# The first feed-forward layer's modulation made in four quarters of the features, and the tokens loaded ahead of the weights on one queue

## The chip, the cores and the metric

One core of one Trainium2 chip. The metric is the device time of one execution in microseconds (us), the median of a few runs; the profile shows one further execution of the same program, with its own time. Engines as the profile names them: PE multiplies matrices (PEld is its weight load, which overlaps), DVE and ACT work on vectors, POOL is the general-purpose engine, SP only issues transfers (DMAs). Each engine takes its instructions strictly in program order, and they meet through semaphores.

## The reference, cut to what matters

Two layers, three sublayers each, on 384 tokens (two tiles of 128 latent tokens, one tile of 128 context tokens) of 1024 features. Only the very first sublayer's start is touched:

```python
mod = silu(cond) @ w_ada[i] + b_ada[i]            # cond = c (latent) or c_ctx (context)
h = rmsnorm(x, norm_pre) * (1 + scale) + shift     # scale, shift: 1024 columns each of mod
a, b = split(h @ w_in)                             # w_in: 1024 x 5632
out = (silu(a) * b) @ w_out                        # w_out: 2816 x 1024
```

So before the first product of the kernel can run, the modulation needs 2048 columns of `w_ada` (8 MB), the tokens (1.5 MB), their norms, and their transposes.

## The kernel before, in words

**Weights.** All weights stream through one ordered list `chunks` of 512 KB pieces, issued by SP (`w_dma`, L172) into a rotating set of raw buffers (`raw_of`; the first `NE` chunks rotate over ten buffers, the later ones over the three `raws`). Chunks in the set `plain` (the `w_ada` ones) are used as they are. Every other chunk is split by `w_split`: ACT makes a rounded high part `wh` (L198), DVE (or POOL, where `ws["eng"]` is `G`) makes the low part `wl` (L199). There are five `wh`/`wl` pairs (`NW`). `take` hands out the next chunk and splits it if that has not been done; `prefetch(n)` splits up to n chunks ahead. A raw buffer's next transfer is issued once its last reader is done; SP's queue is in order, so it waits there.

**Products.** A product is made of three matmuls of 384 columns (high x high, high x low, low x high: L451 to L453, or L461 to L466). A chunk of the first feed-forward layer holds 4 blocks of 128 features and 256 output columns, that is 8 products or 24 matmuls. Chunk (g, kp) is output group g, features 0 to 511 for kp 0 and 1, features 512 to 1023 for kp 2 and 3; kp 0 and 2 carry `a`, kp 1 and 3 carry `b`. The text also names the first eight by the names in the changed code: f00, f01, f02, f03 are group 0 with kp 0 to 3, and f10 to f13 group 1.

**The start (`start`).** Tokens come by POOL's queue (L1407). Each tile is squared (ACT L365), gets its factor from POOL (L358, L359), is scaled by DVE (L1471) and transposed on PE (`lay`, L434). `gather` (L1428) multiplies a `w_ada` chunk with the two condition vectors; the sums lie in four strips of a PSUM bank, which ACT copies (L1430); `spread` (L1437) adds the strips and turns them into columns, and DVE finishes scale and shift (L1443, L1447). `modulate_first` applies them: DVE scales (L1458), ACT makes the high part of `hT` (L1463), DVE the low part (L1467). This is done in two halves of the features: 8 `w_ada` chunks, features 0 to 511, three feed-forward chunks' products, with the other 8 `w_ada` chunks in between (`between`), then features 512 to 1023 and the other products of the first two groups. From the ninth chunk on the layer runs chunk after chunk.

**Background work.** The modulations of the later sublayers are made by DVE on the side: `pace` is called 50 times in the first layer, and in all 80 units (`ada_unit`, DVE L245 and L247, fed by POOL's transfers) are spread evenly over the calls. A "kind" is 16 units; two calls after its last unit PE sums it with four matmuls against ones (`ada_step`, L272). Five kinds belong to the first layer. `pace` is called once per chunk in the first matrix product from where the loop goes on after `between`, and once per 128 rows (k) of the second one (`project_out`). In there, k = 0 to 13 run for all tokens, the last eight chunks are kept and used tile by tile (`block`), and five splits of weights more than usual are done from k = 9 on.

## Time and profile before

| | |
|---|---|
| time, median of 3 runs | 1585.67 us (1583.9 to 1587.08) |
| the profiled execution: time, span | 1587.23 us, 1585.5 us |
| PE busy | 1549.3 us, 98% of the span |
| DVE, ACT, POOL busy | 66%, 41%, 10% |
| end of the first eight feed-forward chunks | 71.98 us from the span's start |

Time from the span's start is used throughout. A row of the timeline gives start, length, engine, line, operation, output <- inputs, shape and count; what stands in brackets is the idle time before it and what ended it. Matmuls overlap, so the pace of a series is read from the starts, not from the lengths.

### The profile page before, as it was taken

How to read it: one execution, taken by the hardware profiler on the slowest of the kernel's cores; microseconds unless marked ns; L12 is line 12 of the kernel's file. 1: busy time of each engine (PE TensorE's matmuls, PEld its weight loads, DVE VectorE, ACT ScalarE, POOL GpSimd, SP SyncE). 2: the span in 40 equal slices, each digit the busy share in tenths (PEclk: the TensorE clock that was granted, in tenths of full speed). 3: DMA queues.
4: the chain of work that ended last, by engine and by line, in shares of the span. 5: the costliest groups of instructions: out<-in, count | busy, mean ns of one | idle time of the engine just before them, and what ended most of it. 6: DMA issues, size and time to landing. Idle time of an engine off the chain costs nothing.

```text
span 1585.5 us, 22547 instructions
## 1 busy us (share of the span) xinstructions
PE 1549.3 (98%) x8798; PEld 1414.8 (89%) x8798; DVE 1046.4 (66%) x1388; ACT 651.6 (41%) x1118; POOL 161.7 (10%) x308
## 2 busy tenths in 40 slices
PE   6999999998999999999999999999999999999997
PEld 4899998887879999988999998899999889999985
DVE  3787788577756777785688889666666764333452
ACT  3423233365745322334523233356655443323441
POOL 1111111000011111120111111110000110000000
PEclk9999999999999999999999999999999999999999
DMA  8777667342224766665377776634333335433321
GB/s 307 245 242 219 221 214 239 120 146 81 67 94 138 218 216 206 207 215 180 114 235 228 227 236 229 227 106 134 101 113 100 121 113 163 130 126 127 131 96 40
DMA packets 164091, 264.50 MB, mean 167 GB/s; under 512 B 10432, under 2 KB 122144, under 8 KB 163984
## 3 DMA queue, kind: packets, MB, share of 16 engines
q1 hardware_dynamic: 140592, 187.27, 36.4%
q0 software_dynamic: 22864, 75.36, 14.8%
q8 instruction: 69, 1.13, 0.3%
q10 hardware_dynamic: 528, 0.43, 0.1%
q14 instruction: 38, 0.31, 0.1%
HBM read 260.01 MB, written 3.01 MB: 166 GB/s over the span
## 4 chain that ended last, share of the span: by engine, by line
PE 92%; DVE 4%; ACT 2%; issue 1%; DMA 0%; POOL 0%; DVEq 0%; POOLq 0%; ACTq 0%
PE pb L451 14%; PE pb L452 14%; PE pb L453 14%; PE pb L461 14%; PE pb L463 13%; PE pb L466 13%; PE pb L963 1%; PE pb L272 1%; PE pb L953 1%; PE pb L923 1%; PE pb L1132 1%; DVE slot L247 1%; PE pb L434 1%; DVE wl L199 1%; PE pb L1428 1%
## 5 line engine op out<-in xcount | busy, mean ns | idle before, releaser
L198 ACT ACTIVATE wh<-raw 128x1024 fp32r<-128x1024 f32 x247 | 259.8, 1058 | 413.2 <-PE pb L466 254.8
L461 PE MATMUL pb<-hT,wh 128*128 128x384 f32 (+1 forms) x1248 | 410.2, 332 | 0.0
L199 DVE TENSOR_TENSOR wl<-raw,wh 128x1024 fp32r<-128x1024 f32 x245 | 298.5, 1223 | 167.7 <-ACT wh L198 167.2
L463 PE MATMUL pb<-hT,wl 128*128 128x384 f32 (+1 forms) x1248 | 406.5, 329 | 0.0
L247 DVE SCALAR_TENSOR_TENSOR slot<-araw,sc,slot 128x1024 f32<-128x1024 f32 x224 | 281.5, 1279 | 0.0
L466 PE MATMUL pb<-hT,wh 128*128 128x384 f32 (+1 forms) x1248 | 259.8, 329 | 0.0
L461 PEld LDWEIGHTS pb<-hT,wh 128*128 128x128 f32 x1248 | 234.8, 188 | 6.2 <-issue 5.9
L463 PEld LDWEIGHTS pb<-hT,wl 128*128 128x128 f32 x1248 | 234.9, 188 | 0.2
L466 PEld LDWEIGHTS pb<-hT,wh 128*128 128x128 f32 x1248 | 215.8, 188 | 0.0
L451 PE MATMUL pb<-wh,gh 128*128 128x512 f32 x384 | 150.6, 392 | 0.2 <-DVE dump L282 0.2
L452 PE MATMUL pb<-wl,gh 128*128 128x512 f32 x384 | 149.6, 389 | 0.0
L453 PE MATMUL pb<-wh,gl 128*128 128x512 f32 x384 | 149.5, 389 | 0.0
L233 POOL DMA_DIRECT2D araw<-in_w_ada_dram x128 | 68.7, 537 | 578.0 <-DVE slot L247 480.6
L451 PE MATMUL pb<-hT,wh 128*128 128x384 f32 x352 | 119.7, 340 | 4.9 <-ACT hT L1463 4.9
L452 PE MATMUL pb<-hT,wh 128*128 128x384 f32 x352 | 119.0, 338 | 0.2 <-DVE hT L1467 0.2
L453 PE MATMUL pb<-hT,wl 128*128 128x384 f32 x352 | 118.6, 337 | 0.0
L199 DVE TENSOR_TENSOR wl<-araw,wh 128x1024 fp32r<-128x1024 f32 x52 | 63.6, 1224 | 68.3 <-ACT wh L198 68.3
L451 PE MATMUL pb<-wh,hT 128*128 128x512 f32 (+1 forms) x258 | 94.3, 365 | 1.1 <-ACT sgn L1242 0.9
L453 PE MATMUL pb<-wh,hT 128*128 128x512 f32 (+1 forms) x258 | 90.7, 352 | 0.0
L452 PE MATMUL pb<-wl,hT 128*128 128x512 f32 (+1 forms) x258 | 90.6, 351 | 0.0
L451 PEld LDWEIGHTS pb<-wh,gh 128*128 128x128 f32 x384 | 72.1, 188 | 19.4 <-issue 3.4
L453 PEld LDWEIGHTS pb<-wh,gl 128*128 128x128 f32 x384 | 72.1, 188 | 15.2
(242 smaller groups left out, 2177.8 us busy)
## 6 DMA issues: line engine op xcount, KB each, us to landing
raw<-in_w_ffn_in_dram SPq DMA_DIRECT2D x155, 512.0 KB, 4.4
araw<-in_w_ada_dram POOLq DMA_DIRECT2D x128, 512.0 KB, 4.4
raw<-in_w_ffn_out_dram SPq DMA_DIRECT2D x76, 512.0 KB, 4.2
raw<-in_w_rec_in_dram SPq DMA_DIRECT2D x21, 512.0 KB, 3.6
araw<-in_w_ffn_in_dram SPq DMA_DIRECT2D x21, 512.0 KB, 3.5
araw<-in_w_rec_in_dram SPq DMA_DIRECT2D x19, 512.0 KB, 3.7
slot<-dsc POOLq DMA_DIRECT2D x24, 256.0 KB, 5.2
raw<-in_w_qkv_dram SPq DMA_DIRECT2D x12, 512.0 KB, 4.1
```

What stands on the lines that cost most here:

```text
L198: S.activation(out=h, in_=r, func=AF.Copy)
L199: ws["eng"].tensor_tensor(out=lo, in0=r, in1=h.bitcast(F32), op=ALU.subtract)
L233: G.dma_start(out=araw[j % NA], in_=w_ada[kd[0], (j % 8) * P:(j % 8 + 1) * P, acol(kd):acol(kd) + 1024])
L247: V.scalar_tensor_tensor(out=acc[v], in0=src, scalar=s_, in1=acc[v], op0=ALU.mult, op1=ALU.add)
L272: T.matmul(out=bank[32 * r:32 * r + 32, :], lhsT=ones, rhs=acc[v][:, 512 * h:512 * h + 512], start=True, stop=True, skip_group_check=True,)
L434: T.transpose(bks[half][:, k * P:(k + 1) * P], src[:, kk * P:(kk + 1) * P], ident)
L451: T.matmul(out=out, lhsT=a[0], rhs=b[0], start=start, stop=False, skip_group_check=True)
L452: T.matmul(out=out, lhsT=a[0], rhs=b[1], start=False, stop=False, skip_group_check=True)
L453: T.matmul(out=out, lhsT=a[1], rhs=b[0], start=False, stop=stop, skip_group_check=True)
L461: T.matmul(out=out, lhsT=a[0], rhs=b[0], start=start, stop=False, skip_group_check=True)
L463: T.matmul(out=out, lhsT=x, rhs=y, start=False, stop=False, skip_group_check=True)
L466: T.matmul(out=out, lhsT=x, rhs=y, start=False, stop=stop, skip_group_check=True)
```

## The change

The modulation is made in four quarters of 256 features. A quarter needs four `w_ada` chunks of 256 columns (two for scale, two for shift; a chunk is now four blocks of 128 rows by 256 columns), which come as one `gather` each of four matmuls of 256 columns. The order of the chunks is: four `w_ada` chunks, f00, f01; four, f10, f11; four, f02, f03; four, f12, f13. `unit` runs two feature blocks of one output tile (6 matmuls); every quarter of the features has 8 units. `NE` goes from 18 to 22. The tokens are loaded by SP's queue ahead of all weights. `between` holds the written order, the gates of both groups included, and the loop goes on with n = 8 where it went on with n = 3.

```diff
-NE = 18
-PLAIN = tuple(range(8)) + tuple(range(10, 18))
+NE = 22
+PLAIN = tuple(6 * q + i for q in range(4) for i in range(4))
...
+    order = add_ffn(0, 0)
+    early_chunks = []
+    for q in range(4):
         for kind in (1, 0):
-            for q in range(4):
-                col = kind * 1024 + half * 512
-                chunks.append(av[0][:, 2 * q:2 * q + 2, col:col + 512])
...
+            col = kind * 1024 + 256 * q
+            early_chunks += [av[0][:, 4 * h:4 * h + 4, col:col + 256] for h in range(2)]
+        early_chunks += chunks[4 * (q % 2) + 2 * (q // 2):][:2]
+    chunks[0:8] = early_chunks
...
+            def unit(gi, s, m, w, kq):
+                wv = [a.rearrange("p (k n) -> p k n", k=4) for a in w]
+                ms = slice(m * P, m * P + P)
+                group = []
+                for k in (2 * kq, 2 * kq + 1):
+                    group.append((bank(gi, m, s)[:, 0:TOK], (wv[0][:, k % 4, ms], wv[1][:, k % 4, ms]), (hT[:, :, 0, k, :], hT[:, :, 1, k, :]),
+                                  k == 0, k == KD - 1))
+                mm3s(group, "a")
...
-                    between(fill)
+                    between(unit, gate)
                     prefetch()
-                    n = 3
+                    n = 8
...
-        w_dma()
         SP.dma_start(out=cf[:, 0:P + 2], in_=cst_f[:, 0:P + 2])
         for t in range(2):
-            G.dma_start(out=x[t], in_=x_sample[0, t * P:(t + 1) * P, :])
-        G.dma_start(out=x[2], in_=x_prompt[0])
+            SP.dma_start(out=x[t], in_=x_sample[0, t * P:(t + 1) * P, :])
+        SP.dma_start(out=x[2], in_=x_prompt[0])
         w_ahead()
...
+        def gather(q, i, ahead=3):
+            kind, h = 1 - i // 2, i % 2
             (w,) = take()
+            for k4 in range(4):
+                r = slice(32 * k4, 32 * k4 + 2)
+                T.matmul(
+                    out=PB[7][r, 256 * kind:256 * kind + 256], lhsT=sc[:, :, 4 * h + k4], rhs=w[0][:, 256 * k4:256 * k4 + 256],
+                    start=h == 0, stop=h == 1, skip_group_check=True,
+                )
+            if i == 3:
+                S.activation(out=mrw[q % 2], in_=PB[7], func=AF.Copy)
...
+        def between(unit, gate):
+            ws["eng"] = G
+            (f00,) = take()
+            ws["eng"] = V
+            modulate_first(0)
+            (f01,) = take()
+            laid(1)
+            for s, w in ((0, f00), (1, f01)):
+                for m in range(2):
+                    unit(0, s, m, w, 0)
+            for i in range(4):
+                gather(1, i, 0)
+            (f10,) = take()
+            unit(1, 0, 0, f10, 0)
+            spread(1)
+            unit(1, 0, 1, f10, 0)
             modulate_first(1)
+            (f11,) = take()
+            unit(1, 1, 0, f11, 0)
+            for m in range(2):
+                unit(0, 0, m, f00, 1)
+            for i in range(4):
+                gather(2, i, 0)
+            for m in range(2):
+                unit(0, 1, m, f01, 1)
+            spread(2)
+            for s, m, w in ((0, 0, f10), (0, 1, f10), (1, 0, f11)):
+                unit(1, s, m, w, 1)
+            (f02,) = take()
+            modulate_first(2)
+            (f03,) = take()
+            for s, w in ((0, f02), (1, f03)):
+                for m in range(2):
+                    unit(0, s, m, w, 2)
+            for i in range(4):
+                gather(3, i, 0)
+            (f12,) = take()
+            for m in range(2):
+                unit(1, 0, m, f12, 2)
+            spread(3)
+            modulate_first(3)
+            for kq in range(2):
+                unit(1, 1, 1, f11, kq)
+            (f13,) = take()
+            w_split(24, 12)
+            for s, w in ((0, f02), (1, f03)):
+                for m in range(2):
+                    unit(0, s, m, w, 3)
+            gate(0, TOK)
+            w_split(26, 18)
+            for m in range(2):
+                unit(1, 1, m, f13, 2)
+            for s, w in ((0, f12), (1, f13)):
+                for m in range(2):
+                    unit(1, s, m, w, 3)
+            gate(1, TOK)
```

Three places of the changed order are shown. Lines of the changed program lie three below (helpers) or up to 17 below (`start`) those of before: L195 and L196 are the old L198 and L199, L1411 the old L1428, L1416 the old L1430, L1425 the old L1437, L1454 the old L1463, L244 the old L247, L269 the old L272.

**First place: ACT after the second set of gathers.** Before, where PE has begun the second half's gathers (L1430 is the copy of the gathered sums, L198 a high part of weights):

```order
L198 ACTIVATE wh_98<-raw_95 128x1024 [waits DMAHW7_49]
L1481 ACTIVATE slot_113<-pb_67 128x4x128
L1430 ACTIVATE slot_111<-pb_71 128x512 [waits PE_49]
L198 ACTIVATE wh_99<-raw_94 128x1024 [waits DMAHW0_49]
L1430 ACTIVATE slot_111<-pb_70 128x512 [waits PE_49,Activation_49]
L198 ACTIVATE wh_100<-raw_95 128x1024 [waits DMAHW1_49]
L198 ACTIVATE wh_101<-raw_96 128x1024 [waits DMAHW2_49]
```

And with the change, after the first quarter's `hT` (wh_99 is f10, wh_100 is f11):

```order
L195 ACTIVATE wh_98<-araw_108 128x1024 [waits DMAHW6_49]
L1472 ACTIVATE slot_113<-pb_67 128x4x128
L1416 ACTIVATE slot_111<-pb_71 128x512 [waits PE_49]
L195 ACTIVATE wh_99<-raw_96 128x1024 [waits DMAHW3_49]
L1454 ACTIVATE hT<-slot_112 128x2x128 [waits DVE_49]
L1454 ACTIVATE hT<-slot_114 128x128 [waits DVE_49]
L1454 ACTIVATE hT<-slot_112 128x2x128 [waits DVE_49]
L1454 ACTIVATE hT<-slot_114 128x128 [waits DVE_49]
L195 ACTIVATE wh_100<-slot_115 128x1024 [waits DMAHW4_49]
```

The high part of f10 stands right behind the copy that waits for PE's gathers, and that of f11 behind the second quarter's `hT`; before, two more copies of sums and three high parts stood together ahead of the second half's `hT`.

**Second place: PE at the last gathers, and SP's transfers for them.** Before, PE between two halves (wh_99 is the third chunk, raw_94 holds it):

```order
L1428 MATMUL pb_70<-araw_108,sc 2x512 x2
L1437 MATMUL pb_71<-cf,slot_111 128x2 x4
L1428 MATMUL pb_70<-araw_109,sc 2x512 x2
L1428 MATMUL pb_70<-gbr,sc 2x512 x2
L451 MATMUL pb_68<-hT,wh_99 128x384
L452 MATMUL pb_68<-hT,wh_99 128x384
L453 MATMUL pb_68<-hT,wl_104 128x384
```

With the change, PE at the fourth quarter (wh_98 is f12, which is loaded into raw_95):

```order
L1411 MATMUL pb_71<-raw_94,sc 2x256 x4
L1411 MATMUL pb_71<-raw_95,sc 2x256 x4
L1411 MATMUL pb_71<-raw_96,sc 2x256 x4
L1411 MATMUL pb_71<-slot_115,sc 2x256 x4
L458 MATMUL pb_68<-hT,wh_98 128x384
L460 MATMUL pb_68<-hT,wh_98 128x384
```

And SP's queue there (the first four are the fourth quarter's `w_ada` chunks, then f12, f13 and the ninth chunk):

```order
L169 DMA raw_94<-in_w_ada_dram 128x4x256 [waits DMAHW3_49,PE_49]
L169 DMA raw_95<-in_w_ada_dram 128x4x256 [waits DMAHW4_49,PE_49]
L169 DMA raw_96<-in_w_ada_dram 128x4x256 [waits DMAHW5_49,DVE_49]
L169 DMA slot_115<-in_w_ada_dram 128x4x256 [waits DMAHW6_49,DVE_49]
L169 DMA raw_95<-in_w_ffn_in_dram 128x4x256 [waits DMAHW7_49,DMAHW4_49,PE_49]
L169 DMA raw_96<-in_w_ffn_in_dram 128x4x256 [waits DMAHW5_49,DMAHW0_49,PE_49]
L169 DMA raw_94<-in_w_ffn_in_dram 128x4x256 [waits DMAHW3_49,DMAHW1_49]
```

The products that use f12 stand right behind the gathers, and f12's transfer waits for PE to have read raw_95 in the second of these four gathers.

**Third place: DVE and PE at the fifth kind's end, in `project_out`.** Before, DVE's last rows ahead of the tile-by-tile part (gl_295, gl_296 are the low parts that k = 12, 13 make ready):

```order
L633 TENSOR_TENSOR gl_295<-g_late,gh_287 128x384
L199 TENSOR_TENSOR hT<-raw_94,hT 128x1024
L199 TENSOR_TENSOR hT<-raw_95,hT 128x1024
L633 TENSOR_TENSOR gl_296<-g_late,gh_288 128x384
L199 TENSOR_TENSOR wl_105<-raw_96,wh_100 128x1024
L199 TENSOR_TENSOR wl_106<-raw_94,wh_101 128x1024
```

With the change, the same stretch of DVE:

```order
L636 TENSOR_TENSOR gl_252<-g_late,gh_244 128x384
L196 TENSOR_TENSOR hT<-raw_94,hT 128x1024
L196 TENSOR_TENSOR hT<-raw_95,hT 128x1024
L244 SCALAR_TENSOR_TENSOR slot_115<-araw_109,sc,slot_115 128x1024
L244 SCALAR_TENSOR_TENSOR slot_116<-araw_109,sc,slot_116 128x1024
L636 TENSOR_TENSOR gl_253<-g_late,gh_245 128x384
L196 TENSOR_TENSOR wl_105<-raw_96,wh_100 128x1024
L196 TENSOR_TENSOR wl_106<-raw_94,wh_101 128x1024
L244 SCALAR_TENSOR_TENSOR slot_115<-araw_107,sc,slot_115 128x1024
L244 SCALAR_TENSOR_TENSOR slot_116<-araw_107,sc,slot_116 128x1024
```

And PE, 12 matmuls behind the start of the first tile's block (before, the fifth kind's L272 stood in k = 9):

```order
L448 MATMUL pb_67<-eh_2031,gh_248 128x512
L449 MATMUL pb_67<-el_2032,gh_248 128x512
L450 MATMUL pb_67<-eh_2031,gl_256 128x512
L269 MATMUL pb_64<-slot_115,ones 32x512 x2
L269 MATMUL pb_64<-slot_116,ones 32x512 x2
L448 MATMUL pb_66<-eh_2033,gh_241 128x512
```

Since the loop goes on five chunks later, the 80 units of the background work end five k later: eight units (four of which are shown) now lie in k = 9 to 13 between the splits, and PE's sum of the fifth kind waits for the last of them.

## Rows read from the trace of the kernel before

**Rows 1.** The page: busy time of each engine with its share of the span, and the chain that ended last, by engine.
```profile
PE 1549.3 (98%) x8798; PEld 1414.8 (89%) x8798; DVE 1046.4 (66%) x1388; ACT 651.6 (41%) x1118; POOL 161.7 (10%) x308
PE 92%; DVE 4%; ACT 2%; issue 1%; DMA 0%; POOL 0%; DVEq 0%; POOLq 0%; ACTq 0%
```

**Rows 2.** The waits of PE from 50 to 330 us, all of them: who waited for whom, us in total, times, longest.
```profile
PE pb L451 <- ACT hT L1463: 1.7, 1, 1.7
PE pb L452 <- DVE hT L1467: 0.2, 1, 0.2
PE pb L451 <- DVE dump L282: 0.2, 1, 0.2
```

**Rows 3.** Timeline of PE to the first products: gathers L1428, transposes L434, the first product.
```profile
7.64 1.88 PE L1428 MATMUL pb<-raw,sc 128*2 128x512 f32 x4 [0.27 <-DVE sc L1419]
13.82 1.97 PE L434 MATMUL pb<-cf,slot 128*128 128x128 f32 x8
16.96 1.09 PE L434 MATMUL pb<-cf,slot 128*128 128x128 f32 x8
21.55 1.03 PE L1428 MATMUL pb<-gbr,sc 128*2 128x512 f32 x4
27.49 0.69 PE L451 MATMUL pb<-hT,wh 128*128 128x384 f32 x1 [3.17 <-ACT hT L1463]
```

**Rows 4.** Timeline of PE from the second half's gathers to the end of the eighth chunk: first and last of the eight gathers, spread, the products behind them, and two products 102 matmuls (34 rows of L451) apart.
```profile
38.73 0.60 PE L1428 MATMUL pb<-raw,sc 128*2 128x512 f32 x2
43.38 0.44 PE L451 MATMUL pb<-hT,wh 128*128 128x384 f32 x1
45.58 0.95 PE L1437 MATMUL pb<-cf,slot 128*128 128x2 f32 x8
50.43 0.45 PE L451 MATMUL pb<-hT,wh 128*128 128x384 f32 x1 [1.71 <-ACT hT L1463]
54.30 0.33 PE L451 MATMUL pb<-hT,wh 128*128 128x384 f32 x1
71.98 0.33 PE L451 MATMUL pb<-hT,wh 128*128 128x384 f32 x1
```

**Rows 5.** Timeline of the other engines at the start: token square and scaling, copy of sums, high part and low part of weights, the modulation beside POOL's low part and without it.
```profile
6.88 0.63 ACT L365 ACTIVATE dump<-x 128x512 f32<-128x512 f32 x1 [3.99 <-DMA x<-in_x_sample_dram]
9.30 0.75 DVE L1471 TENSOR_SCALAR slot<-x,stat 128x1024 f32<-128x1024 f32 x1 [1.72 <-POOL stat L359]
24.24 2.34 POOL L199 TENSOR_TENSOR wl<-raw,wh 128x1024 fp32r<-128x1024 f32 x1 [10.57 <-ACT wh L198]
24.64 2.93 DVE L1458 TENSOR_SCALAR slot<-slot,slot 128x256 f32<-128x256 f32 x4
40.70 0.60 ACT L1430 ACTIVATE slot<-pb 128x512 f32<-128x512 f32 x1 [9.07 <-PE pb L1428]
41.19 1.05 ACT L198 ACTIVATE wh<-raw 128x1024 fp32r<-128x1024 f32 x1
42.27 1.22 DVE L199 TENSOR_TENSOR wl<-raw,wh 128x1024 fp32r<-128x1024 f32 x1 [8.68 <-ACT wh L198]
43.61 0.17 DVE L1447 SCALAR_TENSOR_TENSOR slot<-slot 128x8 f32<-128x8 f32 x1
50.95 0.66 DVE L1458 TENSOR_SCALAR slot<-slot,slot 128x256 f32<-128x256 f32 x2
51.39 0.62 ACT L1463 ACTIVATE hT<-slot 128x256 fp32r<-128x256 f32 x2 [0.50 <-DVE slot L1458]
51.53 0.62 DVE L1467 TENSOR_TENSOR hT<-slot,hT 128x256 fp32r<-128x256 f32 x2
```

**Rows 6.** Transfers: the one weight chunk issued alone between 38 and 42 us, with its time from issue to landing; and what the DMA engines moved in three stretches (last column GB/s): `w_ada` chunks with 2 KB rows and tokens in the first two, two feed-forward chunks with 1 KB rows among them in the third.
```profile
L172 SPq DMA_DIRECT2D raw<-in_w_ffn_in_dram x1: 367/367/367, 39.8 to 39.8; - x1
DMA to landing us min/median/max: 3.4/3.4/3.4
4.00:14.00 10.00, 6.02 (x18) 2.12 (x19) 1.97 (x4) 4.00 (x12) 2.60 (x6) 1.00 1.04 395
14.00:18.00 4.00, 4.00 (x24) 2.54 (x26) 1.69 (x5) 0.00 (x0) 0.00 (x0) 1.00 1.05 387
18.00:22.00 4.00, 3.31 (x29) 1.35 (x28) 0.68 (x3) 1.08 (x2) 0.00 (x0) 1.00 1.09 359
```

**Rows 7.** The granted clock of PE (third column from the right; 1.00 is 2.4 GHz, 0.50 is 1.2 GHz) in short stretches around idle times of PE; the first number behind the length is PE's busy time. One row of PE's timeline follows, the end of the idle time at 1234.
```profile
26.00:26.20 0.20, 0.00 (x0) 0.00 (x0) 0.20 (x1) 0.00 (x0) 0.20 (x1) 0.98 1.09 399
26.20:26.40 0.20, 0.00 (x0) 0.00 (x0) 0.20 (x1) 0.00 (x0) 0.20 (x1) 0.50 1.05 389
32.00:33.00 1.00, 1.00 (x5) 1.00 (x4) 1.00 (x3) 0.00 (x0) 0.00 (x0) 0.50 1.08 361
33.00:34.00 1.00, 1.00 (x8) 1.00 (x7) 0.60 (x1) 0.00 (x0) 0.00 (x0) 0.99 0.94 273
50.00:50.50 0.50, 0.07 (x1) 0.07 (x1) 0.50 (x3) 0.50 (x3) 0.50 (x2) 1.00 0.91 283
1234.00:1235.00 1.00, 0.48 (x2) 0.49 (x3) 1.00 (x3) 0.00 (x0) 0.00 (x0) 0.76 0.16 20
1237.00:1238.00 1.00, 1.00 (x4) 0.80 (x3) 0.29 (x1) 1.00 (x2) 0.00 (x0) 0.54 0.29 78
1234.52 1.65 PE L1132 MATMUL pb<-qd,ki 128*128 128x128 f32 x6 [2.15 <-DVE am L1134]
```

**Rows 8.** Timeline in `project_out`, from k = 9 to the tile-by-tile part: DVE's last two background units (L247), its first and last operations from k = 9 on, ACT's first of k = 9 and of the eight kept chunks, and PE's sum of the fifth kind and first matmul on the kept chunks.
```profile
263.19 2.48 DVE L247 SCALAR_TENSOR_TENSOR slot<-araw,sc,slot 128x1024 f32<-128x1024 f32 x2
264.62 0.53 ACT L632 ACTIVATE gh<-g_late 128x384 fp32r<-128x384 f32 x1 [2.60 <-PE pb L452]
265.58 0.55 DVE L633 TENSOR_TENSOR gl<-g_late,gh 128x384 fp32r<-128x384 f32 x1
286.50 1.23 DVE L199 TENSOR_TENSOR wl<-raw,wh 128x1024 fp32r<-128x1024 f32 x1 [1.19 <-ACT wh L198]
267.46 1.07 PE L272 MATMUL pb<-slot,ones 128*32 128x512 f32 x8
286.71 0.39 PE L451 MATMUL pb<-eh,gh 128*128 128x512 f32 x1
286.94 0.39 PE L452 MATMUL pb<-el,gh 128*128 128x512 f32 x1
```

More of the change, by code (lines that the diff above doesn't have):

```diff
@@ L663, in ffn @@
             n = 0
-            todo = order if between is None else first
             while n < len(order):
-                gi, kp = todo[n]
+                gi, kp = order[n]
                 if n == len(order) - 2:
@@ L705, in ffn @@
                 prefetch()
-                products(gi, kp, w, 0, NT, side=n == 3 and between is not None)
+                products(gi, kp, w, 0, NT)
                 if n == 4 and between is None:
@@ L1398, in start @@
         G.memset(mhalf, -0.5)
-        for kind in range(2):
-            V.memset(PB[6 + kind], 0.0)
+        V.memset(PB[7], 0.0)
         S.activation(out=stat[:, 0, :], in_=ones[:, 0:8], func=AF.Silu)
@@ L1483, in laid @@
                     V.tensor_copy(out=dst, in_=src)
-        normalise(0)
-        normalise(1)
-        w_split(1, 0)
-        normalise(2)
-        for q in range(4):
-            gather(1, q)
-            if q < NT:
-                lay(q)
-            else:
-                laid(0)
-            if q == 1:
+        for t in range(NT):
+            normalise(t)
+        for i in range(4):
+            gather(0, i, (3, 2, 1, 0)[i])
+            if i < NT:
+                lay(i)
+            if i == 1:
                 T.transpose(PB[6][:, 0:56], rows2, ident[0:56, 0:56])
@@ L1498, in start @@
                 V.tensor_copy(out=lg, in_=PB[6][:, 24:56])
[L1499 to L1521 removed]
+        laid(0)
```

97 lines of the change are left out of this document (26 added, 71 removed).

## The prediction

> **What bounds the kernel now.** I read the page first: PE is busy for 98% of the span and holds 92% of the chain that ended last [rows 1]. The waits come next: from 50 to 330 us PE waits 2.1 us in all [rows 2]. So whatever moves the end of the first eight feed-forward chunks, now at 71.98 us [rows 4], moves the end of the kernel one for one, unless a new wait appears later. The timeline of the first 72 us shows how PE gets there: gathers and transposes, 3.2 us idle, the first product at 27.49 [rows 3], the second half's gathers from 38.73, 1.7 us idle, the remaining products from 50.43 [rows 4]. The change adds no matmul work: a gather has 4 x 256 columns for 2 x 512, there are still 16 of them and four spreads. What can be gained is an earlier first product; what can be lost is waits between products.
>
> **The first product.** SP issues the first token tile at about 2.0 us. Alone, 512 KB land 3.4 us after issue [rows 6], so 5.4 us, and the next ones 1.33 us apart at 395 GB/s: the first `w_ada` chunk at 9.4. Chunks of 1 KB rows look slower (359 GB/s with some of them under way [rows 6]); at that rate the fourth lands at about 14. The token path takes 3.2 us from landing to the scaled tile (6.88 to 9.30 + 0.75 [rows 5]), so the tiles are ready at 8.7, 10.1 and 11.4. PE's own work ends last: gather, transposes, gather, transposes, at the half clock that [rows 3] still show at 13.82 and no longer at 16.96 (0.95 per gather at 1.88 for two, 1.97 per tile), run from 9.4 to 15.3. With the clock up, which I assume after some 6 us of work as before, a small transpose, a gather (0.5), transposes (1.09) and a gather bring it to 17.9. Before, the last gather ended at 21.55 + 1.03 = 22.58 and the first product started 4.9 us later [rows 3]: copy, spread, modulation, the latter held up by POOL's low part (four DVE operations took 2.93 us beside it, two take 0.66 without [rows 5]). The same chain, plus one ACT copy of transposes (0.5) now standing ahead of the weights' high part, gives the first product at **23.3**, 4.2 us earlier.
>
> Here the Trainium skill has a rule (SBUF — State Buffer, section "SBUF: two separate sides"): DVE and POOL lock the port they share, and whichever starts first keeps it for the whole instruction. The trace agrees with 2.93 us against 0.66. Were DVE free of that hold, the first product would come at 21.2, which I keep as the early end.
>
> **From there to the end of the eighth chunk,** PE in its new order. A unit of six matmuls takes 1.04 us, since 102 matmuls run from 54.30 to 71.98, 0.173 each [rows 4]. Four gathers take 1.85 ((43.38 - 38.73 - 0.95 for a spread) / 8 each), a spread 0.95 [rows 4].
> - Quarter 1, 4 units: after the idle time before it PE runs 5.5 us at half clock, as from 27.49 to 33.0 [rows 3, 7], 16 matmuls, then 8 more: 30.2.
> - Gathers: 32.1. The next unit uses f10, whose high part stands on ACT behind the copy of these gathers' sums: from 40.70 copy and high part took 1.54, with DVE's low part 2.79 [rows 5]. PE starts at 33.7 and waits again for the low part: 35.3, **2.2 lost**. Spread, unit: 37.3.
> - f11's high part stands behind the second quarter's `hT`: three small DVE operations from 36.35 (0.2 each), two pairs of scalings, two pairs of high parts, then 1.05 [rows 5], ready at 39.6; its low part 1.25 later. Unit ends at 41.2, **2.85 lost**.
> - Two units, gathers, two units, spread, three units: 51.4. DVE makes f02's low part ahead of the third quarter's modulation, **0.6 lost**; four units: 56.1. Gathers: 58.0.
> - f12: its transfer waits for the second of these gathers, 57.1; landing 3.4 later, 60.5; high part 61.6; low part 62.8. PE waits 3.6 at once and 0.5 for the low part: **4.1 lost**; nothing covers it, because these products stand next in PE's order and the last spread behind them. Two units end at 64.2, spread 65.2.
> - The next unit writes the bank that DVE is still reading (three operations): **0.7 lost**. Then 12 units: **78.4**.
>
> In sum 23.3 + 33.3 (192 matmuls) + 2.7 (half clock) + 5.55 (12 gathers) + 2.85 (3 spreads) + 10.5 (waits) = 78.2, rounding aside. Against 71.98 that is **+6.4**. DMA hides behind this: 13.5 MB at 359 GB/s are through by about 42 us, except for f12. The gates, the ninth chunk's split and the rest of the move lie beside 10 us of products. POOL's token issues cost nothing.
>
> **The clock.** PE fell to half clock at 26.2, 1.9 us after its last matmul, and at 1234.5 after 2.15 us idle, and stayed there 5.5 and about 3 us of work; an idle time of 1.9 us ended at 50.43 without a fall [rows 7]. f12's 3.6 us therefore costs the clock as well. Two units, a spread and the waits behind them at half rate: I take **+2.0** (the short stretch gives 1.3, the long one 2.7). f11's 2.3 us stands so near the edge that I leave its 1.3 to the range.
>
> The Trainium skill says it as a rule (TensorE: Matmul & The Clock Gate, section "HAM oscillation — how this bites in real kernels"): waits for transfers between groups of matmuls throttle the clock again, and each restart is paid at half rate. That speaks against a change that puts three such waits where there was one. [...]
>
> **The fifth kind.** The 50 calls now end at k = 13. Eight units of about 1.2 us [rows 8] lie in k = 9 to 13 on DVE. From k = 9 (ACT's row at 264.62) five k of 4.08 us (18 matmuls of 0.227, the step from 286.71 to 286.94) and 12 matmuls later PE wants their sum: 23.1 us on. DVE, free at 265.58, has nine splits of 1.15 to 1.23, counted at 1.15, five `gl` of 0.55 and eight units to do [rows 8]: 22.6 us without any idle time, so 23.5 on. It will idle some 2.6 us where a split waits for its raw buffer's transfer (a landing of 4 us behind each freed buffer): 26.1. PE waits **3.0** (0.4 to 4.4), with PE now 1.8 us behind DVE at that sum (267.46 against 265.67). Past 2 us idle the clock falls: **+1.3**, up to 2.7.
>
> **Sum:** 6.4 + 2.0 + 3.0 + 1.3 = +12.7 us. The profiled execution took 1587.23 (span 1585.5 and 1.7 around it), so 1599.9; the median of the runs shown lies 1.56 lower, so **1598.4**. A difference under 0.2% (3.2 us) can hardly be told from no change.
>
> **The rivals.**
> - The waits come, the clock holds and DVE is nearly in time for the fifth kind: 6.4 + 0.4 = +6.8, **1592.5**. For it: the idle time that ended at 50.43; DVE's bound of 0.4. Against: f12's wait is longer than both that dropped the clock. Chance 0.25; the forecast 0.50.
> - The first product comes much earlier: the clock up from the start (transposes 1.09 for 1.97, gathers 0.5: 2.6 us less) and no hold by POOL (2.1): 18.6 instead of 23.3, then 78.4 - 4.7 + 0.4 = +2.1, **1587.8**, not to be told from no change. Against: the row at half clock at 13.82. Chance 0.10.
> - Faster: the high parts are ready when PE reaches them, so that the three waits for weights (2.2, 2.85 and 4.1) vanish and nothing else changes: 6.4 - 9.15 + 0.4 = -2.4; with the early first product -7.1, **1578.6**. It decides once these waits together fall under 3 us. Against: the rows of ACT's order, in which each high part stands behind a wait on PE or on `hT`, and SP's row for f12. Chance 0.07.
> - The change doesn't bring its early start: the tokens ahead of the weights hold up the first gathers as much as the smaller quarter saves, the first product stays near 27.5: +4.2 more, **1602.6**. For it: nothing in PE's queue can pass the first gather. Against: only 3.7 MB, for 5.8, must land first. Chance 0.08.
>
> **How the numbers follow.** Slower holds the forecast, the first and the last rival, 0.83; same 0.10; faster 0.07. The range leaves out the fast rival and what lies beyond the unknown costs: from 1587 (the early first product) to 1606 (the forecast with f11's 1.3, the fifth kind's upper ends, and 3 us of start). The forecast's own range is 1594 to 1606.
>
> **What would show it.** The first product near 23.3; PE idle before f10, f11 and f12 of about 1.6, 2.3 and 3.6 us, each ended by ACT's high part; half clock behind f12; the ninth chunk's first matmul at 78 to 81 for 71.98; PE waiting for DVE before the fifth kind's sum. It is wrong if the ninth chunk starts before 72, or if the waits sit elsewhere, on gathers whose chunks have not landed above all.

## The result and the profile after

The changed kernel takes 1605.93 us (median of 4 runs, 1604.47 to 1606.65) where the kernel before took 1586.38 beside it: ratio 1.0128, 95% interval 1.0115 to 1.0140, that is about 20 us slower. 1598.4 was predicted. The profiled execution took 1605.28 us with a span of 1603.5, against 1587.23 and 1585.5 before.

The page first: engine busy times, the chain that ended last, and the granted clock in 40 slices of the span.

```profile
PE 1554.6 (97%) x8862; PEld 1421.8 (89%) x8862; DVE 1045.2 (65%) x1394; ACT 651.3 (41%) x1118; POOL 158.1 (10%) x304
PE 90%; DVE 4%; ACT 2%; issue 2%; DMA 1%; POOL 0%; SPq 0%; DVEq 0%; POOLq 0%; ACTq 0%
PEclk8899999999999999999999999999999999999998
```

The same last line of the page before:

```profile
PEclk9999999999999999999999999999999999999999
```

The averages say almost nothing: PE still holds 90% of the chain [rows 1 showed 92%]. What the reader is to see is the clock of the first two slices. All waits of PE from 20 to 330 us (who waited for whom, us in total, times, longest), to be read against [rows 2]:

```profile
PE pb L458 <- ACT wh L195: 8.7, 3, 6.0
PE pb L458 <- ACT hT L1454: 3.6, 1, 3.6
PE pb L269 <- DVE slot L244: 2.5, 1, 2.5
PE pb L448 <- DVE c L298: 1.0, 1, 1.0
PE pb L458 <- DVE slot L1435: 0.5, 1, 0.5
PE pb L463 <- DVE wl L196: 0.3, 1, 0.3
```

The 8.7 us behind ACT's high parts are the waits for f10, f11 and f12. PE's timeline has them one by one: first gather, first product (which answers to the last of [rows 3]), f10, the spread behind it, f11, the gathers of the third and fourth quarters, f12, the spread and the bank wait behind it, and the ninth chunk, which stood at 71.98 in [rows 4].

```profile
10.09 1.03 PE L1411 MATMUL pb<-raw,sc 128*2 128x256 f32 x8 [6.30 <-DMA raw<-in_w_ada_dram]
23.00 0.69 PE L458 MATMUL pb<-hT,wh 128*128 128x384 f32 x1 [3.59 <-ACT hT L1454]
33.57 0.44 PE L458 MATMUL pb<-hT,wh 128*128 128x384 f32 x1 [1.66 <-ACT wh L195]
35.41 1.70 PE L1425 MATMUL pb<-cf,slot 128*128 128x2 f32 x8
40.25 0.69 PE L458 MATMUL pb<-hT,wh 128*128 128x384 f32 x1 [1.01 <-ACT wh L195]
45.90 1.05 PE L1411 MATMUL pb<-slot,sc 128*2 128x256 f32 x16
58.68 1.48 PE L1411 MATMUL pb<-raw,sc 128*2 128x256 f32 x24
66.61 0.69 PE L458 MATMUL pb<-hT,wh 128*128 128x384 f32 x1 [6.02 <-ACT wh L195]
70.61 1.70 PE L1425 MATMUL pb<-cf,slot 128*128 128x2 f32 x8
72.83 0.69 PE L458 MATMUL pb<-hT,wh 128*128 128x384 f32 x1 [0.52 <-DVE slot L1435]
86.92 0.33 PE L448 MATMUL pb<-hT,wh 128*128 128x384 f32 x1
```

The two spreads took 1.70 us where the spread of [rows 4] took 0.95: half clock. The windows (granted clock third from the right) show how long it lasted, from about 35.1 to 45.4 and, counted from f12's first product, from 66.6 to 76.1:

```profile
35.00:36.00 1.00, 1.00 (x6) 1.00 (x6) 0.00 (x0) 0.00 (x0) 0.00 (x0) 0.55 0.96 244
36.00:40.00 4.00, 3.24 (x12) 2.73 (x11) 2.71 (x11) 1.94 (x5) 0.00 (x0) 0.50 0.98 337
40.00:44.00 4.00, 3.75 (x12) 3.63 (x13) 1.22 (x1) 0.20 (x1) 0.00 (x0) 0.50 0.42 123
68.00:72.00 4.00, 4.00 (x17) 4.00 (x16) 0.00 (x0) 0.00 (x0) 0.00 (x0) 0.50 0.44 131
72.00:76.00 4.00, 3.48 (x12) 3.39 (x13) 3.28 (x12) 2.14 (x5) 0.00 (x0) 0.50 0.00 0
76.00:80.00 4.00, 4.00 (x25) 4.00 (x24) 1.98 (x3) 2.76 (x4) 0.00 (x0) 0.99 0.47 142
```

f12's 6.02 us are longer than the prediction's landing time explains. The timeline of POOL, SP and ACT there (three transfers each of POOL and SP in one row):

```profile
56.41 0.95 POOL L1548 MEMSET gbr<- 128x1024 f32 x1 [34.26 <-DVE wl L196]
57.31 1.83 POOL L230 DMA_DIRECT2D araw<-in_w_ada_dram  x3
59.78 1.50 SPq L169 DMA_DIRECT2D raw<-in_w_ffn_in_dram  x3
65.50 1.06 ACT L195 ACTIVATE wh<-raw 128x1024 fp32r<-128x1024 f32 x1 [4.19 <-DMA raw<-in_w_ffn_in_dram]
```

And SP's line from 59.5 to 60.0, where f12 is its only transfer, with the time from issue to landing:

```profile
L169 SPq DMA_DIRECT2D raw<-in_w_ffn_in_dram x1: 368/368/368, 59.8 to 59.8; - x1
DMA to landing us min/median/max: 5.7/5.7/5.7
```

The first three transfers of the background work, 512 KB each, start 1.2 to 2.5 us ahead of f12, and two further chunks of SP's queue follow it within 1 us. So f12 lands 5.7 us after its issue, where a chunk alone took 3.4 [rows 6].

The rest of the loss lies in the second matrix product: a product that waits for DVE's copy of the fourth kind's columns (L298), and the fifth kind's sum.

```profile
243.70 0.50 PE L448 MATMUL pb<-wh,gh 128*128 128x512 f32 x1 [1.04 <-DVE c L298]
306.19 2.25 PE L269 MATMUL pb<-slot,ones 128*32 128x512 f32 x8 [2.47 <-DVE slot L244]
```

The sum over the profiled executions: 14.94 to the ninth chunk, 2.47 and 1.04 here, 18.45 in all. The span grew by 18.0. Before, the clock fell at 1234 and cost some 1.5 us [rows 7]; in this execution the same idle time of 2.15 us, at 1253.91, left the clock at 1.00. The other way about 1.1 us are left over; the fifth kind's sum itself shows 2.25 us for 1.07 [rows 8], which makes them up. No run shows why that sum takes longer; the clock stood at 1.00 in it.

### The profile page after: what moved, and what is told of

Read it like the earlier page. It is cut to its first block, busy times and chain, and to the rows that moved or that the text cites. A ratio compares the mean times of both kernels' runs of the same rounds, so it can differ in the third digit from the quotient of the medians.

```text
span 1603.5 us, 22679 instructions
## 1 busy us (share of the span) xinstructions
PE 1554.6 (97%) x8862; PEld 1421.8 (89%) x8862; DVE 1045.2 (65%) x1394; ACT 651.3 (41%) x1118; POOL 158.1 (10%) x304
## 4 chain that ended last, share of the span: by engine, by line
PE 90%; DVE 4%; ACT 2%; issue 2%; DMA 1%; POOL 0%; SPq 0%; DVEq 0%; POOLq 0%; ACTq 0%
PE pb L458 14%; PE pb L460 14%; PE pb L463 14%; PE pb L448 13%; PE pb L450 13%; PE pb L449 13%; PE pb L950 1%; DVE slot L244 1%; PE pb L269 1%; PE pb L940 1%; DVE wl L196 1%; PE pb L910 1%; PE pb L1119 1%; PE pb L431 1%; ACT wh L195 1%
## 5 line engine op out<-in xcount | busy, mean ns | idle before, releaser
L458 PE MATMUL pb<-hT,wh 128*128 128x384 f32 (+1 forms) x1312 | 436.9, 336 | 12.8 <-ACT wh L195 8.7
L195 ACT ACTIVATE wh<-raw 128x1024 fp32r<-128x1024 f32 x242 | 254.6, 1058 | 407.9 <-PE pb L463 257.4
L460 PE MATMUL pb<-hT,wl 128*128 128x384 f32 (+1 forms) x1248 | 406.5, 329 | 0.0
L196 DVE TENSOR_TENSOR wl<-raw,wh 128x1024 fp32r<-128x1024 f32 x242 | 294.5, 1223 | 166.9 <-ACT wh L195 164.2
L244 DVE SCALAR_TENSOR_TENSOR slot<-araw,sc,slot 128x1024 f32<-128x1024 f32 x224 | 281.1, 1278 | 0.0
L458 PEld LDWEIGHTS pb<-hT,wh 128*128 128x128 f32 x1312 | 249.8, 190 | 21.2 <-ACT wh L195 10.2
L463 PE MATMUL pb<-hT,wh 128*128 128x384 f32 (+1 forms) x1248 | 259.8, 329 | 0.0
L460 PEld LDWEIGHTS pb<-hT,wl 128*128 128x128 f32 x1248 | 234.9, 188 | 0.2
L463 PEld LDWEIGHTS pb<-hT,wh 128*128 128x128 f32 x1248 | 215.8, 188 | 0.0
L196 DVE TENSOR_TENSOR wl<-araw,wh 128x1024 fp32r<-128x1024 f32 x54 | 66.0, 1224 | 68.6 <-ACT wh L195 68.6
L448 PE MATMUL pb<-hT,wh 128*128 128x384 f32 x288 | 96.7, 336 | 0.0
L450 PE MATMUL pb<-hT,wl 128*128 128x384 f32 x288 | 96.3, 334 | 0.0
L449 PE MATMUL pb<-hT,wh 128*128 128x384 f32 x288 | 96.3, 334 | 0.0
```

What stands on the lines that cost most here:

```text
L195: S.activation(out=h, in_=r, func=AF.Copy)
L196: ws["eng"].tensor_tensor(out=lo, in0=r, in1=h.bitcast(F32), op=ALU.subtract)
L244: V.scalar_tensor_tensor(out=acc[v], in0=src, scalar=s_, in1=acc[v], op0=ALU.mult, op1=ALU.add)
L448: T.matmul(out=out, lhsT=a[0], rhs=b[0], start=start, stop=False, skip_group_check=True)
L449: T.matmul(out=out, lhsT=a[0], rhs=b[1], start=False, stop=False, skip_group_check=True)
L450: T.matmul(out=out, lhsT=a[1], rhs=b[0], start=False, stop=stop, skip_group_check=True)
```

## The experiments

All kernels were timed beside the kernel before. "Ninth chunk" is its first matmul in the profiled execution. An execution's start shifts by up to 1.2 us from one to the next (first gather at 9.83 to 11.07 with the same start), so differences behind the first product say more than the positions. In the kernels with `split_early` (below) lines lie 12 further down: L470, L472, L475 for L458, L460, L463, and L199 for L195.

| kernel | first product | f10, f11, f12 wait | ninth chunk | median us | ratio to before (95%) |
|---|---|---|---|---|---|
| before | 27.49 | none | 71.98 | 1584.3 to 1586.4 | 1 |
| the change | 23.00 | 1.66, 1.01, 6.02 | 86.92 | 1605.93 | 1.0128 (1.0115 to 1.0140) |
| f10 ahead | 22.61 | 0, 2.06, 6.15 | 84.22 | 1606.07 | 1.0133 (1.0118 to 1.0148) |
| f10, f11 ahead | 22.80 | 0, 0, 6.97 | 81.17 | 1602.01 | 1.0110 (1.0095 to 1.0125) |
| f12 in a free buffer | 22.67 | 1.66, 1.02, 1.72 | 78.72 | 1600.85 | 1.0104 (1.0088 to 1.0121) |
| POOL later | 23.93 | 1.66, 1.02, 4.79 | 84.95 | 1603.89 | 1.0123 (1.0107 to 1.0139) |
| 45 calls | 23.03 | 1.66, 1.01, 5.91 | 84.28 | 1601.43 | 1.0100 (1.0083 to 1.0118) |
| tokens first, alone | 27.45 | none | 72.54 | 1587.95 | 1.0014 (1.0005 to 1.0023) |
| tokens back | 21.78 | 1.66, 1.02, 6.05 | 85.60 | 1604.91 | 1.0121 (1.0107 to 1.0135) |
| waits gone | 23.99 | 0, 0, 0 | 70.82 | 1586.07 | 0.9998 (0.9990 to 1.0007) |
| and f00 on DVE | 21.87 | 0, 0, 0 | 68.86 | 1584.44 | 0.9992 (0.9983 to 1.0001) |
| and tokens back | 20.67 | 0, 0, 0 | 67.61 | 1583.23 | 0.9980 (0.9971 to 0.9989) |
| the change, busy wait | 24.13 | 1.66, 1.01, 0.78 + 1.01 | 84.84 | 1606.36 | 1.0130 (1.0116 to 1.0143) |
| the best, busy wait | 21.16 | 0, 0, 0 | 66.38 | 1582.34 | 0.9984 (0.9975 to 0.9993) |

**f10 ahead.** `split_early` makes the two parts of one chunk at a given place and marks it as done.

```diff
+            split_early(10)
             for i in range(4):
                 gather(1, i, 0)
```

> The changed kernel with f10 alone split as soon as it has landed, ahead of ACT's copy of the second quarter's sums. Theory A (an idle time of PE of 1.7 us or more drops the clock, and the drop costs more than the idle time): f10's 1.66 us and its 0.30 us for the low part go, but f11, still split behind the second quarter's hT, now finds PE early: an idle time of some 2.1 us at about 35 for 1.01 at 40.25, and the clock falls there instead. The third set of gathers starts at about 43 for 45.90; time -3 us, 1603. Rival B (the fall at 35 does not come from the idle time but from what PE runs there, the spread and the small gathers): the half clock starts at about 34 as before, gathers at 44, -2 us. Rival C (1.66 us was the only idle time that counts): no fall at all before 60 us, gathers at 40.3, -5.6 us, 1600.

PE's idle time moved to f11, as theory A and the prediction's 2.3 us had it. PE's timeline:

```profile
36.46 0.44 PE L470 MATMUL pb<-hT,wh 128*128 128x384 f32 x1 [2.06 <-ACT wh L199]
```

And the windows behind it:

```profile
36.00:37.00 1.00, 0.54 (x3) 0.54 (x4) 0.70 (x2) 0.41 (x1) 0.00 (x0) 1.00 1.09 363
38.00:40.00 2.00, 2.00 (x7) 2.00 (x8) 0.00 (x0) 0.00 (x0) 0.00 (x0) 0.50 1.09 344
41.00:42.00 1.00, 1.00 (x11) 0.63 (x13) 0.00 (x0) 0.00 (x0) 0.00 (x0) 1.00 0.19 65
```

The clock fell behind that idle time and came back after 3 us instead of 10. The third set of gathers started at 41.77 and the ninth chunk 2.7 us earlier than with the change. The time did not follow: in this execution the clock also fell behind the fifth kind's wait, now 2.88 us, and at 1252.62. Against the changed kernel PE lost 1.3 us at the first place, 0.4 of it the longer wait, and 1.4 at the second. Theory A stands for the mechanism, its 3 us were given back.

**f10 and f11 ahead.** The same with `split_early(11)` behind it.

> The changed kernel with f10 and f11 both split as soon as they have landed. Theory A: no idle time above 0.6 us between 30 and 58 us, so the clock stays at 1.00 from 29 us to f12; the third set of gathers starts at 38 to 39 for 45.90; f12's wait of 6.0 and the half clock behind it stay as they are; time -7 to -8 us, about 1598. Rival B (the clock falls at 35 from what PE runs there): half clock from about 34, gathers at 42 to 43, -3 us, 1603.

Windows from the second gathers' end on:

```profile
30.00:34.00 4.00, 4.00 (x46) 3.15 (x35) 0.44 (x4) 0.60 (x1) 0.00 (x0) 1.00 0.98 310
34.00:38.00 4.00, 3.95 (x22) 3.24 (x20) 2.28 (x8) 1.20 (x4) 0.00 (x0) 1.00 1.02 341
```

And the third set of gathers in PE's timeline:

```profile
38.10 1.05 PE L1423 MATMUL pb<-slot,sc 128*2 128x256 f32 x16
```

Without the idle times the clock stays at 1.00 over the same spread and the same small gathers, so these did not drop it: rival B is out. The gathers come 7.8 us earlier. f12 comes earlier by less: its wait grew to 6.97, and 12 us at half clock follow. The ninth chunk gained 5.75, the time 3 to 4 (by the ratios, by the medians).

**f12 in a free buffer.**

```diff
-NE = 22
+NE = 24
```

> The changed kernel with f12 and f13 loaded into buffers that come free with the third quarter's gathers (NE 24 for 22). Theory A (the wait for f12 and the clock that it drops are 6.0 and about 4.7 us of the loss): PE has no idle time above 1 us behind the gathers at 58.7, the clock stays at 1.00 from 46 us on, the ninth chunk starts at about 76.4 for 87.1; time -10.7 us, 1595. Rival (the wait moves on: DVE's low part and f13 come late in its place, or the clock falls anyway): the ninth chunk at 81, -6 us, 1600.

The transfer is in time, and what shows behind it is ACT's order: f12's high part stands behind the copy of the gathers' sums, which costs PE 1.72 us:

```profile
61.88 0.44 PE L458 MATMUL pb<-hT,wh 128*128 128x384 f32 x1 [1.72 <-ACT wh L195]
```

This time the clock held, by the window behind it:

```profile
64.00:68.00 4.00, 3.48 (x24) 3.39 (x23) 2.31 (x10) 1.47 (x5) 0.00 (x0) 1.00 0.86 278
```

The ninth chunk gained 8.2 us: 4.3 of waiting and 3.9 of half clock. The expected 10.7 missed the 1.72 and took the clock's price 0.8 too high. Of the time 5.1 us came back by the medians (7.0 in the profiled execution, where the clock now fell at 1246). That is the rival's time, and part of the wait did move on, to ACT's high part.

**POOL later.** POOL's memset and background transfers are put behind an operation that reads f12's low part.

```diff
+            G.tensor_tensor(out=r32[:, 0:8], in0=rst[:, 0:8], in1=place[22][1][:, 0:8].bitcast(F32), op=ALU.subtract)
             G.memset(gbr, 0.0)
```

> The changed kernel with POOL's memset and its three background transfers held back until f12 is split. Theory A (f12 took 5.7 us from issue to landing for 3.4 because three background transfers stood ahead of it on the same DMA engines): landing 3.4 to 3.7 us, PE idle 3.7 us for 6.02, the clock falls all the same; time -2.3 us, 1603.6. Rival (f12's neighbours on SP's queue, f13 and the ninth chunk, are what slows it): landing 5.7 as before, no change. Rival that the background transfers, now late, hold up DVE's first units: PE does not wait for these, so nothing.

SP's line at f12's issue, with the landing time:

```profile
L169 SPq DMA_DIRECT2D raw<-in_w_ffn_in_dram x1: 367/367/367, 61.1 to 61.1; - x1
DMA to landing us min/median/max: 4.5/4.5/4.5
```

And PE's first product with f12:

```profile
66.70 0.69 PE L458 MATMUL pb<-hT,wh 128*128 128x384 f32 x1 [4.79 <-ACT wh L195]
```

Half right. f12 lands in 4.5 us in place of 5.7, not in 3.4 (five executions with POOL's transfers ahead have 5.6 to 6.6). So 1.1 us or more were POOL's transfers. The 1.1 us left over the lone chunk's 3.4 fit the rival, f13 and the ninth chunk, which SP issues within 1 us behind f12; that was not tried apart. The median gained the 2 us expected, the profiled execution did not (1607.17): there the fifth kind's wait was 3.42 us, with the clock falling behind it and once more at 1255.

**45 calls.**

```diff
-            set_pace(n_kinds, 36 if (l, sl) == (1, 2) else 50)
+            set_pace(n_kinds, 36 if (l, sl) == (1, 2) else 45 if (l, sl) == (0, 0) else 50)
```

> The changed kernel with the first layer's background units spread over 45 calls for 50, so that they end at k = 8 as before the change. Theory: the wait of 2.5 us for the fifth kind's sum and the 1.0 us behind it (a product that needs the bank which DVE is still copying) both vanish, and the ninth chunk starts at 87 as before; time -3.5 us, 1602.4. Rival (the product loop's chunks have no room for the faster pace, so DVE is late elsewhere): new waits of PE between 90 and 250 us, no gain.

Between 90 and 330 us PE has no wait of 0.2 us or more. Both waits are gone, 3.5 us. The profiled execution gained 6.5: 2.6 of them stand ahead of the ninth chunk, since the half clock behind f12's 5.91 us lasted only 2.9 us of its products. The median gained 4.5 (its runs spread from 1598.82 to 1605.59).

**Tokens first, alone**, in the kernel before, and **tokens back**, in the changed kernel: the same edit in the two directions.

```diff
+        w_dma()
         SP.dma_start(out=cf[:, 0:P + 2], in_=cst_f[:, 0:P + 2])
         for t in range(2):
-            SP.dma_start(out=x[t], in_=x_sample[0, t * P:(t + 1) * P, :])
-        SP.dma_start(out=x[2], in_=x_prompt[0])
+            G.dma_start(out=x[t], in_=x_sample[0, t * P:(t + 1) * P, :])
+        G.dma_start(out=x[2], in_=x_prompt[0])
```

> The kernel before with only the tokens moved ahead of the weights on SP's queue; halves, chunks and order stay. Theory A (what bounds the first half's start is the sum of bytes that must land and PE's own work behind them): the first gather moves from 7.64 to about 10, the first product stays within 0.7 us of 27.49; time the same. Rival B (nothing in PE's queue passes the first gather, so the later gather delays all behind it): first product at 29.5, +2 us. Rival C (the tokens' earlier landing brings the transposes forward): first product at 26, -1.5 us.

> The changed kernel with the tokens back on POOL's queue, beside the weights; the quarters stay. Theory A: the first gather comes at about 7.6 for 10.09, the tokens land about 1 us later for sharing the DMA engines, the first product stays within 1 us of 23.0, time the same within 1 us. Rival B (the early start came from the tokens' place in the queue and not from the smaller quarter): first product at 25 or later, +2 us or more.

The first gather came where expected, at 10.08 alone and at 7.72 back. With the halves the first product did not move (27.45). With the quarters it came 1.2 us earlier with the tokens back on POOL's queue, a little more than theory A allowed; the eight executions with the tokens first and f00's low part on POOL had it at 22.61 to 24.13 (PE's timeline of the kernel with the tokens back):

```profile
7.72 1.03 PE L1412 MATMUL pb<-raw,sc 128*2 128x256 f32 x8 [0.27 <-DVE sc L1405]
21.78 0.69 PE L458 MATMUL pb<-hT,wh 128*128 128x384 f32 x1 [3.59 <-ACT hT L1455]
```

So the smaller quarter brings the early start, and the tokens' place in the queue takes a little of it away: with the weights first PE begins its four gathers and 24 transposes 2.4 us sooner, and about half of that reaches the first product. The times resolve neither well. Alone, the tokens' move cost 0.14% (0.05 to 0.23); in its profiled execution the clock fell behind the 1.68 us ahead of the second half's products, where the 1.71 us of [rows 4] had not dropped it.

**Waits gone.** f10, f11, f12, f13 ahead, `NE` 24, 45 calls together.

```diff
+            split_early(10)
+            split_early(11)
             for i in range(4):
                 gather(1, i, 0)
...
+            split_early(22)
+            split_early(23)
             for i in range(4):
                 gather(3, i, 0)
```

> The changed kernel with f10 to f13 all split as soon as they have landed, f12 and f13 loaded into buffers that come free with the third quarter's gathers, and the background units spread over 45 calls. Theory (all of the loss is these waits and the clock behind them): no idle time of PE above 0.8 us between the first product at 23.0 and 330 us, no half clock behind 29 us, the ninth chunk at 68 to 70 for 71.98 before and 87.1 with the change; time 2 to 4 us under the kernel before, 1582.5 to 1584.5 where that one takes 1586.4. Rival (the smaller chunks or the written order cost something of their own): the ninth chunk at 74 or later, time above that of the kernel before.

All waits of PE from 30 to 330 us:

```profile
PE pb L470 <- DVE slot L1447: 0.6, 1, 0.6
PE pb L307 <- DMA r<-dsc: 0.2, 1, 0.2
```

And the windows that hold f10's and f12's first products, behind which the changed kernel ran at half clock:

```profile
30.00:40.00 10.00, 9.95 (x82) 7.76 (x84) 2.91 (x12) 1.80 (x5) 0.00 (x0) 1.00 0.88 282
50.00:60.00 10.00, 9.41 (x78) 7.98 (x77) 4.74 (x13) 2.71 (x6) 2.72 (x4) 1.00 0.74 261
```

All 20 us come back, and the kernel is level with the one before. From the first product to the ninth chunk it takes 46.8 us, with the change 63.9. So the waits and the clock behind them are the whole loss, and the smaller chunks and the written order cost nothing that shows. The expected gain of 2 to 4 us did not come: of the 1.2 us that the ninth chunk is ahead of the kernel before, 0.9 are lost again by attention's first wait (379.19 for 379.48). Some 0.6 of this goes at one place near 228 us, where a sum of the background work takes 2.15 us (L281) for 1.06 before (L272); why it does is open, as with the fifth kind's sum.

**f00 on DVE** (`split_early(4)` ahead of the first quarter's last gather), and **the tokens back** as well.

> The kernel with all waits gone, and f00 also split early, ahead of ACT's copy of the first sums, its low part on DVE instead of POOL. Theory (POOL's low part holds DVE up by 1.8 us at 20.05, four operations in 3.09 us for 1.25): the first product moves from 23.0 to 24.0 down to 21.2 to 22.2, 1.8 us behind the start of the modulation less than before, and the ninth chunk from 70.8 to 69; time -1.8 us against the kernel with all waits gone, 1584.3. Rival (ACT's high part now stands ahead of the copy and waits for f00's landing, so that the copy comes late): the first product not earlier, time the same.

> The same with the tokens back on POOL's queue. Theory (in the changed kernel this brought the first product from 23.0 to 21.78): first product at 20 to 21, the ninth chunk at 67.5 to 68.5 for 71.98 before; time 3 us under that of the kernel before. Rival (with less time ahead of it, PE now waits for transfers, the second quarter's weights above all): the ninth chunk at 70 or later, no gain against the version with the tokens first.

DVE's four scalings beside POOL's low part, in the timeline of the changed kernel:

```profile
20.05 3.09 DVE L1449 TENSOR_SCALAR slot<-slot,slot 128x256 f32<-128x256 f32 x4
```

And without it, in the timeline of the kernel with f00 on DVE:

```profile
20.75 1.25 DVE L1461 TENSOR_SCALAR slot<-slot,slot 128x256 f32<-128x256 f32 x4
```

The prediction kept a first product at 21.2 as the early end if DVE were free of that hold. PE's wait for the first `hT` fell from 3.59 to 2.17 us; the two edits together put the first product at 20.67. With both, the kernel takes 1583.23 us, 0.20% under the kernel before (0.11 to 0.29): the change's idea does pay once nothing waits, by 3 us.

**The change, busy wait**: 24 products whose results are thrown away, in the wait for f12.

```diff
             (f12,) = take()
+            for i in range(24):
+                T.matmul(out=PB[7][:, 0:TOK], lhsT=f11[0][:, 0:P], rhs=hT[:, :, 0, i % 4, :], start=True, stop=True, skip_group_check=True)
```

> The changed kernel with 24 idle products of 384 columns (4.2 us at full clock, into a bank that is written afresh afterwards) put between the fourth gathers and f12's products, so that PE is busy through most of the wait for f12, which itself stays: f12's high part ends at about 66.6 as before. Theory A (the clock behind f12 is the price of the idle time): idle times of about 1.1 and 0.8 us in place of 6.02, the clock stays at 1.00, and the ninth chunk starts at 82.0 to 82.5 for 86.9; time -4.7 us, 1601. Rival B (the half clock has another cause than the idle time): the clock falls as before, the ninth chunk at 86.9, the time the same. Rival C (a fall of 1.1 us of idle time ahead of the idle products is enough): half clock during them, they end at 70 instead, and the ninth chunk at 87 or later.

PE's timeline, the idle products (L1527) and the first product with f12:

```profile
62.57 4.46 PE L1527 MATMUL pb<-hT,wh 128*128 128x384 f32 x24 [0.78 <-ACT slot L1416]
68.03 0.44 PE L458 MATMUL pb<-hT,wh 128*128 128x384 f32 x1 [1.01 <-ACT wh L195]
```

And the window behind it:

```profile
66.00:70.00 4.00, 2.70 (x14) 2.06 (x14) 1.22 (x1) 1.06 (x1) 0.00 (x0) 1.00 0.81 258
```

f12 is as late as ever, and the clock holds: from its first product to the ninth chunk 16.8 us pass, with the change 20.3. So theory A is right, and the half clock was the price of the idle time. It cost 3.5 us here (3.8 with the wait of 0.3 for the low part that full speed brings out), not the 4.7 expected. As with f10 ahead, the median shows nothing of it, so the expected 1601 was missed: here too the clock fell behind the fifth kind (2.74 us) and at 1254.92, and in attention at 405 as well, where the longest wait was 1.38 us. In the changed kernel's execution it fell at none of the three.

**The best, busy wait**: 11 such products in the wait for the first `hT`.

```diff
+            for i in range(11):
+                T.matmul(out=PB[6][:, 0:TOK], lhsT=f00[0][:, 0:P], rhs=f00[0][:, 0:TOK], start=True, stop=True, skip_group_check=True)
             modulate_first(0)
```

> The version with all waits gone, f00 split by DVE and the tokens on POOL's queue, with 11 idle products of 384 columns (1.9 us at full clock, into a bank that is written afresh afterwards) put into the 2.43 us that PE waits for the first quarter's hT. Theory (the 5.5 us at half clock behind the first product are the price of that idle time, 2.7 us): first product at 20.7 as before, clock 1.00 from there, the second gathers at 25.3 for 27.99, the ninth chunk at 64.9 for 67.6; time -2.7 us against that version, 1580.5 for 1583.2. Rival A (the clock falls all the same): first product and ninth chunk as before, time the same. Rival B (with the earlier products PE meets the second quarter's transfers): gathers at 25.3, but PE idle before them or behind them until about 27, time -1 us or less.

The clock is at 1.00 through the first products, where the other kernels are at 0.50. The window of this kernel:

```profile
21.00:23.00 2.00, 1.75 (x9) 1.20 (x9) 1.70 (x6) 1.99 (x4) 0.00 (x0) 1.00 1.11 350
```

And of the same without the idle products:

```profile
21.00:23.00 2.00, 1.97 (x6) 1.57 (x6) 1.70 (x5) 1.63 (x4) 0.00 (x0) 0.50 1.10 349
```

From the first product to the second gathers it takes 5.6 us for 7.3: 1.7 of the expected 2.7, because PE at full speed overtakes DVE twice (0.25 and 0.37 us). The ninth chunk is 1.2 us earlier; the times, 0.9984 and 0.9980 of the kernel before, don't tell the two apart. In the profiled execution the 1.2 us stand until attention, where the clock now falls at 380.8, among waits of 1.38, 0.49, 0.57 and 1.19 us that leave it at 1.00 in the version without the idle products; 1.1 us are lost there.

## Why the prediction was wrong, step by step

The sign, the places of the waits and the engine that ends each were right; the size was not: +12.7 us against +18.0 in the profiled execution and +20 in the medians.

- **The first product**: 23.3 predicted, 23.00 measured. Right, also that POOL's low part holds up DVE. Only the price of that hold was high: 2.1, where its own rows give 1.6 (2.93 for four operations, 0.66 for two without it); measured 1.8 (3.09 for 1.25).
- **f10**: 1.6 + 0.6 predicted, 1.66 + 0.30 measured. Right.
- **The clock behind f10**: failed. The prediction priced the clock for f12 alone and left f11 to the range, because an idle time had passed without a fall in [rows 7] (1.9 us in its words; the row of [rows 4] has 1.71). The 1.66 us before f10 dropped the clock, in the changed kernel and in all five experiments that keep this wait. The half clock lasted 10 us, 9 of them work: some 4.5 us lost. In return f11's wait shrank from 2.85 to 1.01, since PE was slow enough for it. The fourth set of gathers stood at 58.68 for 56.1.
- **f12**: its transfer was said to land 3.4 us after the issue, as a lone chunk does. It took 5.7. The row used was of a chunk with nothing beside it; the step left out POOL's background transfers, which the same move brings to this very place (the buffer that POOL clears is freed by f03's split), and SP's own two chunks behind. PE's wait was 6.02 for 4.1.
- **The clock behind f12**: predicted, and mis-sized. 2.0 was taken; 9 us of half clock cost about 4.4 in the profile, and the experiment that fills the wait shows 3.5 to 3.8.
- **f02's low part**: 0.6 predicted; no wait of 0.2 us or more stands there, and PE loses some 0.3.
- **The bank wait**: 0.7 predicted, 0.52 measured.
- **The fifth kind**: 3.0 predicted, 2.47 measured. Its fall of the clock, +1.3, did not happen in this execution, so "Past 2 us idle the clock falls" does not hold as a rule: behind the fifth kind it fell with waits of 2.71 to 3.42 us in four experiments, and held with 2.01, 2.14 and this 2.47. The 1.04 us behind L298 was not seen: the fourth kind's last step moves with the pace too.

To the ninth chunk the terms read: first product -0.3, f10 -0.2, its clock +4.5, f11 -1.8, f02 -0.3, f12 +1.9, its clock +2.4, bank wait -0.2. That is 6.0 of the 6.5 by which 86.92 misses 78.4 + 2.0.

The first rival (the waits come, the clock holds) was given 0.25; it is refuted by every run that keeps f10's wait. The two rivals on the start, a first product at 18.6 and one near 27.5, fall with 23.00. The fast rival's condition, high parts ready when PE reaches them, was the right one to name: the version that meets it is level with the kernel before, and ahead once f00's low part and the tokens are moved as well.

The Trainium skill (TensorE: Matmul & The Clock Gate, section "HAM oscillation — how this bites in real kernels") tells of a kernel in which waits for transfers between groups of matmuls throttle the clock again, and each restart is paid at half rate; its waits are some 3 to 5 us long. The runs agree for f12's wait of 6.02 us, and show the same behind a shorter one that ACT ends: 1.66 us of idle time ahead of f10 had 10 us at half clock behind it.

What the prediction took for a licence was one row, with one execution behind it; the runs show that such a row can come out either way.

## What to carry to other kernels

A wait on the engine that sets the end costs its length and the clock behind it: here 4.5 us behind a wait of 1.66, so price both, with a range, and don't take one row in which the clock held as a licence. Before splitting a stage into smaller pieces, follow the queue of each engine that prepares the next piece, and put the preparation ahead of the first instruction that waits for the stage itself; here four splits moved, two buffers changed and a faster pace gave back all 20 us. A transfer's landing time is that of its company: look at what every queue issues in the 3 us around it after the move, not before.
